# The first six quads of an MLP's up product begin with the two products that need only the first half of the tokens

## The chip, the cores and the metric

The kernel runs on one core of one Trainium2 chip. The metric is device time in microseconds from launch to end. A profile of one execution shows when each engine worked: PE (TensorE, the matmuls), DVE (VectorE), ACT (ScalarE), POOL (GpSimd) and SP (SyncE, which issues most of the transfers).

## The reference

```python
def reference(x, ...):                     # x: 1 x 1024 x 1024, float32
    h = x
    for layer in range(2):
        y = _rms_norm(h, mix_norm_g[layer])
        y = mixer(y)                       # layer 0: chunked spatial gating, layer 1: dilated attention
        h = h + y
        y = _rms_norm(h, mlp_norm_g[layer])
        h = h + jnp.square(jax.nn.relu(y @ w_up[layer])) @ w_down[layer]
    return _rms_norm(h, final_norm_g)
```

There are 1024 tokens and a width of 1024; `w_up` of a layer is 1024 x 4096, `w_down` 4096 x 1024. The change lies in `y @ w_up`, in both layers.

## The kernel before, in words

**Layout and precision.** A tile of activations has 128 features on the partitions and 512 tokens (one half of the tokens) along the free axis, float32, 256 KB. A float32 matrix product is made of three matmuls on rounded parts: `split` has ACT copy a tile into its rounded part (`hi`, L202) and has DVE subtract that from the tile (`lo`, L203); `three` then issues hi x hi, hi x lo and lo x hi into one bank, all through the helper `matmul` at L179. So each tile that TensorE reads costs one ACT and one DVE instruction ahead of it.

**The up product.** The 4096 columns of `w_up` are taken as 16 *quads*, q = 0 to 15. A quad is a 2 x 2 block product: its outputs are two blocks of 128 columns (i) by two halves of the tokens (s), its inputs two halves of the 1024 features (j). A block product ("product" below) has four `three`, one for each 128 features k: 12 matmuls of 128x512. A classical quad needs eight products. The scheme of Strassen and Winograd needs seven, on sums and differences of the blocks:

- Left side, `Weights`: four raw tiles of a quad are loaded on SP's queue into pool tag `r`. POOL makes four sums of them (L357, L358, L359 and L362), and seven pairs (`wp`, eight places) are split from raw tiles and sums. `steps` is a generator that does a piece of this at each call; the call `more()` in the loop over quads sets where the pieces of the next quad stand in each engine's order.
- Right side, `Terms`: `first` makes the eight normed tiles of the first half of the tokens (k = 0 to 7; L397 on DVE, kept in `keep`) and splits each (`y`). `second` makes those of the second half, and for each of the four k the tiles t1 and t2 (products 5 and 6; L416 and L417 on DVE), and on POOL (L418, L419) the tiles from which `rest` splits t3 and t4 (products 7 and 4). Products 1 and 2 read the first half's tiles 0 to 3 and 4 to 7, product 3 the second half's tiles 4 to 7.
- Results: the seven products are added up by ACT and DVE, squared behind a ReLU (`squared`, L654 and L655), combined into seven tiles for the down product (`hidden_terms`) and stored to DRAM on SP's queue (`kept`).

**Quads 0 and 1 are classical.** The sums t1 to t4 need all the tokens, and their norm comes late, since the residual of the second half ends just ahead. So quads 0 and 1 do eight products each: first the four blocks (q, i) on the first half of the tokens in four PSUM banks, tile by tile, then the same on the second half. Each tile is used four times, 12 matmuls. In the mean time `second` and the weights of quad 2 (`up_weights(2)`, all at once) are made. Their eight weights are loaded and split ahead of the MLP (`plain`), in layer 1 in two calls during the attention. From quad 2 on there are seven products, in the order 5, 6, 1, 7, 3, 2, 4.

**What sets the order.** The order of PE's instructions is the order in which the program emits them. Work beside it is emitted by generators that `flow` resumes at a due time: each yields an estimate in ns (`LAT`) of when its result will be there, and `flow.until` resumes them when PE needs it. The other engines' orders come from a list scheduler that goes by the order of emission and by priorities (`tc.high_priority` moves an instruction ahead by 60). PSUM has eight banks: three of tag `mm`, five of tag `at`.

Of the kernel before, what the change touches and what calls it, by code (L numbers as in the profile page):

```python
# [17 lines left out]
P = 128  # L18
# [89 lines left out]
LAT = dict(sum=2600.0, rms=2600.0, tile=1600.0, gate=8500.0, soft=4200.0, turn=3800.0, fe=1300.0, v=2000.0, qk=2700.0, merge=2600.0, out=700.0, fex=3.0, ve=1600.0)  # L108
# [3 lines left out]
def trunk(ctx: ExitStack, tc: tile.TileContext, xT, w_u, w_v, w_o, w_s, b_s, w_qkv, w_bo, rel,  # L112
# [225 lines left out]
    class Weights:  # L338
# [12 lines left out]

        def steps(self):
# [4 lines left out]
            tt(r3, r[0, 0], r[1, 0], op=ALU.subtract)  # L357
            tt(r[1, 0], r[1, 0], r[1, 1], op=ALU.add)  # L358
            tt(r[1, 1], r[1, 0], r[0, 0], op=ALU.subtract)  # L359
            yield  # L360
            self.split(1, r[0, 0])
            tt(r[0, 0], r[0, 1], r[1, 1], op=ALU.subtract)  # L362
            yield
            for p, src in ((5, r[1, 0]), (6, r[1, 1]), (7, r3), (3, r[0, 0]), (2, r[0, 1])):
                self.split(p, src)
                yield

    def ahead(w):

        it = w.steps() if w else iter(())  # L370
        return lambda: next(it, None)

    def plain(layer, q):
        w = {}
        for j in range(2):
            for i in range(2):
                w[i, j] = wpair().split(load(w_up[layer, q, i, j]))
        return w

    class Terms:  # L380


        def __init__(self):
            self.blocks = {(j, s): [] for j in range(2) for s in range(2)}
            self.t = {1: self.blocks[0, 0], 2: self.blocks[1, 0], 3: self.blocks[1, 1], 4: [], 5: [], 6: [], 7: []}
            self.kept = []
# [15 lines left out]
        def second(self, sq, gi):  # L402
# [4 lines left out]
            for k in range(4):  # L407
                y, x, (y0, y1) = [], [], (self.kept[k][:, j, :] for j in range(2))
                for j in range(2):
                    o = 4 * j + k  # L410
                    t = raw()
                    nc.vector.scalar_tensor_tensor(t, h[o][:, sq.cols], vec[:, gi, o:o + 1], pb, op0=ALU.mult, op1=ALU.mult)
# [4 lines left out]
                tt(t2, y[1], t1, op=ALU.subtract)  # L417
                nc.gpsimd.tensor_tensor(y0, y[1], y[0], op=ALU.subtract)  # L418
                nc.gpsimd.tensor_tensor(y1, y1, t2, op=ALU.subtract)  # L419
                yield 2 * LAT["tile"]  # L420
                for j in range(2):
# [181 lines left out]
    for tiles in ((0, 1), (2,), (3,), (4, 5, 6, 7)):  # L603
        w = [weight(w_o[m]) for m in tiles]
        for s in range(2):
# [5 lines left out]
            if tiles[-1] == 7:  # L611
                start_terms(sq[s], s, 1, terms)
                if s == 0:
                    first = [plain(0, q) for q in range(2)]
# [18 lines left out]
    def hidden_terms(q, c11, c21, c12, c22, t2, store=True):  # L633
# [4 lines left out]
        if store:  # L638
            kept(q, {1: c11, 3: c22, 7: t3, 5: c12})
# [7 lines left out]
    def mlp(layer, x, first, last):  # L647


        def up_weights(q):  # L650
            return Weights(lambda i, j: w_up[layer, q, i, j])


        tiles = [(q, i) for q in range(2) for i in range(2)]  # L654
        c = {}  # L655
        for s in range(2):
            banks = [at_bank() if (n < 2) == (s == 1) else mm_bank() for n in range(4)]
            if s == 0:
                banks = [mm_bank() if n < 3 else at_bank() for n in range(4)]
            order = [(j, k) for j in range(2) for k in range(4)] if s == 0 else [(j, k) for k in range(4) for j in range(2)]  # L660
            for n, (j, k) in enumerate(order):
                xs = x.blocks[j, s]
                flow.until(lambda: len(xs) > k)
                for b, (q, i) in zip(banks, tiles):
                    three(b, first[q][i, j], blk(k), xs[k], n == 0, n == 7)
                    flow.pump()
            for b, (q, i) in zip(banks, tiles):
                c[q, i, s] = temp()
                with tc.high_priority(offset=PRIO):
                    squared(c[q, i, s], b)  # L670
                if s and i:
                    hidden_terms(q, c[q, 0, 0], c[q, 1, 0], c[q, 0, 1], c[q, 1, 1], c[q, 0, 0])
            if s == 0:
                w = up_weights(2)
                for _ in w.steps():
                    pass
        x.rest()

        for q in range(2, 16):
# [46 lines left out]
            if q < 14:  # L726
                hidden_terms(q, c11, c21, c12, c22, u)
# [559 lines left out]
    for i in range(2):  # L1287
# [6 lines left out]
        if i == 0:  # L1294
            first = [plain(1, 0)]
# [13 lines left out]
    first.append(plain(1, 1))  # L1309
# [89 lines left out]
```

## Time and profile before

| | us |
|---|---|
| runs, in order | 2202.96, 2199.22, 2202.74 |
| median of the three | 2202.74 |
| profiled execution | 2198.1 |
| its span in the profile | 2196.1 |
| PE busy | 2147.9 (98% of the span) |
| DVE busy | 1560.3 (71%) |
| ACT busy | 1103.5 (50%) |
| POOL busy | 507.8 (23%) |

The profiled execution took 2.0 us more than its span, which runs from the first to the last recorded instruction. All numbers of the trace are from this one execution. In rows of a view in order of time, the first number is when a group of like instructions began (us from the span's start), the second how long the group took, then engine, source line, operation, the tile written and the tiles read, shape and count; in square brackets stands the idle time of that engine ahead of the group, and what ended it. A row of a window has the window, its length, then busy time and number of instructions of PE, PEld (weight load), DVE, ACT and POOL, the granted TensorE clock, the DMA share and GB/s.

### The profile page before, as it was taken

Reading aid. Unit: us, or ns where it says so; the run is one execution under the profiler, and the core shown is the slowest. Engines: PE = TensorE matmul, PEld = TensorE weight load, DVE = VectorE, ACT = ScalarE, POOL = GpSimd, SP = SyncE. Lnnn points to the kernel's source line nnn. Section 1 sums busy time; section 2 is a strip of 40 time slices with the busy share of each in tenths; the row PEclk is TensorE's granted clock in tenths of the full one; section 3 lists DMA queues with packets and bytes.
Section 4 is the critical chain, followed back from the end, with each engine's and each line's share of the span. In section 5 each row is a group of like instructions: output and inputs, shape, how many; then the busy total and the mean of one; then the engine's idle time right before and its main releaser. Section 6 shows DMA issues by size and latency. Waiting matters only on the chain.

```text
span 2196.1 us, 30296 instructions
## 1 busy us (share of the span) xinstructions
PE 2147.9 (98%) x10378; PEld 1775.1 (81%) x10378; DVE 1560.3 (71%) x2851; ACT 1103.5 (50%) x2225; POOL 507.8 (23%) x372
## 2 busy tenths in 40 slices
PE   8999999999999999999999999999999999999997
PEld 6888887888878888778888888887778888788886
DVE  6875278777688887775664745647987777888867
ACT  6644145555564443355544545556555556544432
POOL 1100124333223333510000000001433332333344
PEclk9999999999999999999999999999999999999999
DMA  6321104444355443301111111121154443544432
GB/s 221 112 79 50 39 22 160 159 158 146 123 181 161 153 154 116 106 31 40 44 41 44 35 31 50 31 45 30 39 183 154 154 154 124 192 147 151 149 92 96
DMA packets 152334, 230.27 MB, mean 105 GB/s; under 512 B 32761, under 2 KB 47220, under 8 KB 152180
## 3 DMA queue, kind: packets, MB, share of 16 engines
q1 hardware_dynamic: 151280, 227.11, 33.0%
q8 instruction: 81, 1.33, 0.3%
q10 hardware_dynamic: 900, 1.23, 0.2%
q14 instruction: 73, 0.60, 0.1%
HBM read 170.45 MB, written 57.84 MB: 104 GB/s over the span
## 4 chain that ended last, share of the span: by engine, by line
PE 86%; DVE 7%; ACT 2%; DMA 2%; issue 2%; POOL 1%; SPq 0%; DVEq 0%; POOLq 0%; ACTq 0%
PE mm L179 43%; PE at L179 41%; PE at L186 2%; DVE wp L203 1%; DVE y L203 1%; DMA r<-in_w_v 1%; DVE h L300 0%; DVE t L203 0%; DVE h L791 0%; ACT t L1047 0%; DVE t L1322 0%; ACT wp L202 0%; POOL r L358 0%; POOL t L357 0%; DMA t<-hid 0%
## 5 line engine op out<-in xcount | busy, mean ns | idle before, releaser
L179 PE MATMUL mm<-y,whi 128*128 128x512 f32 x1616 | 508.1, 395 | 1.0 <-DVE h L300 1.0
L202 ACT ACTIVATE wp<-r 128x512 fp32r<-128x512 f32 (+3 forms) x388 | 231.8, 600 | 400.6 <-PE at L179 233.5
L179 PE MATMUL at<-hx,wp 128*128 128x512 f32 x1770 | 416.3, 391 | 1.9 <-DVE h L791 1.8
L179 PEld LDWEIGHTS at<-hx,wp 128*128 128x128 f32 x1770 | 334.2, 189 | 73.3 <-DVE h L791 3.5
L203 DVE TENSOR_TENSOR wp<-r,wp 128x512 fp32r<-128x512 f32 (+3 forms) x388 | 322.7, 835 | 80.2 <-ACT wp L202 77.5
L179 PEld LDWEIGHTS mm<-y,whi 128*128 128x128 f32 x1616 | 296.2, 188 | 62.8 <-DVE h L300 1.4
L179 PE MATMUL mm<-y,wlo 128*128 128x512 f32 x808 | 315.4, 390 | 0.0
L179 PE MATMUL at<-t,wp 128*128 128x512 f32 x1344 | 314.5, 389 | 0.8 <-DVE wp L203 0.7
L179 PEld LDWEIGHTS at<-t,wp 128*128 128x128 f32 x1344 | 252.1, 188 | 53.9 <-DVE wp L203 1.2
L256 POOL TENSOR_TENSOR t<-t 128x512 f32<-128x512 f32 (+1 forms) x66 | 82.6, 1252 | 865.0 <-ACT t L251 853.1
L357 POOL TENSOR_TENSOR t<-r 128x512 f32<-128x512 f32 (+3 forms) x62 | 92.2, 1487 | 607.4 <-DMA r<-in_w_up 181.7
L179 PE MATMUL mm<-y,wp 128*128 128x512 f32 x912 | 223.2, 390 | 0.4 <-DVE y L203 0.2
L179 PEld LDWEIGHTS mm<-y,wp 128*128 128x128 f32 x912 | 171.0, 188 | 37.6 <-issue 0.6
L179 PE MATMUL mm<-hx,wp 128*128 128x512 f32 x708 | 172.2, 390 | 7.8 <-DVE b L812 4.7
L179 PEld LDWEIGHTS mm<-y,wlo 128*128 128x128 f32 x808 | 151.7, 188 | 33.0
L203 DVE TENSOR_TENSOR wlo<-r,whi 128x512 fp32r<-128x512 f32 x160 | 113.9, 734 | 77.9 <-ACT whi L202 77.6
L179 PEld LDWEIGHTS mm<-hx,wp 128*128 128x128 f32 x708 | 132.5, 188 | 37.1 <-ACT wp L202 5.0
L202 ACT ACTIVATE whi<-r 128x512 fp32r<-128x512 f32 x160 | 97.3, 626 | 122.2 <-PE mm L179 91.1
L203 DVE TENSOR_TENSOR hx<-t,hx 128x512 fp32r<-128x512 f32 x192 | 142.1, 743 | 0.5 <-ACT hx L202 0.5
L791 DVE TENSOR_TENSOR h<-h,at 128x512 f32<-128x512 f32 x144 | 97.7, 682 | 57.1 <-PE at L179 57.1
L179 PE MATMUL at<-y,wp 128*128 128x512 f32 x480 | 120.7, 394 | 4.8 <-ACT t L688 4.1
L202 ACT ACTIVATE hx<-t 128x512 fp32r<-128x512 f32 x192 | 119.5, 630 | 6.7 <-DMA t<-hid 2.1
(198 smaller groups left out, 3025.7 us busy)
## 6 DMA issues: line engine op xcount, KB each, us to landing
t<-hid SPq DMA_DIRECT2D x182, 256.0 KB, 3.1
hid<-t SPq DMA_DIRECT2D x140, 256.0 KB, 2.3
r<-in_w_up SPq DMA_DIRECT2D x128, 256.0 KB, 2.7
r<-in_w_dn SPq DMA_DIRECT2D x88, 256.0 KB, 2.6
r<-in_w_qkv SPq DMA_DIRECT2D x72, 256.0 KB, 2.7
hid<-b SPq DMA_DIRECT2D x56, 256.0 KB, 2.4
r<-in_w_v SPq DMA_DIRECT2D x48, 256.0 KB, 3.6
h<-in_xT SPq DMA_DIRECT2D x16, 256.0 KB, 5.6
```

Of the source, the lines that this page charges most:

```text
L179: nc.tensor.matmul(out, lhsT, rhs, **kw)
L186: nc.tensor.transpose(out, src, ident)
L202: nc.scalar.activation(hi, src, AF.Copy)
L203: nc.vector.tensor_tensor(lo, src, hi.bitcast(F32), op=ALU.subtract)
L256: nc.gpsimd.tensor_tensor(self.acc, self.acc, sq, op=ALU.add)
L357: tt(r3, r[0, 0], r[1, 0], op=ALU.subtract)
L791: engine.tensor_tensor(hs[i, s], hs[i, s], src, op=ALU.add)
```

## The change

Quads 0 to 5 (`HEAD = 6`) now begin with products 1 and 2, which read the first half's tiles only.

- `half_first` loads and splits two weights of a quad, (0,0) and (0,1), for products 1 and 2. The callers that called `plain` (two quads of four weights) now call it for quads 0 to 3, with the calls at the same places; quads 4 and 5 follow in the up product.
- Two batches of three quads do product 1 of the three and then product 2 of the three, in the three `mm` banks. Behind product 1 ACT copies the bank out (L696): kept in SBUF for quads 0 and 1, stored to DRAM as `p1` for quads 2 to 5. Product 2 goes on in the same bank; that sum is squared and stored at once.
- The classical quads are gone. Between the batches, four POOL sums each for quads 0 and 1 (`sums`) and then, in a hand-written order, the splits of their weights for products 5, 6, 3, 7 and 4. Products 5 and 6 of both quads run interleaved by k; then each quad does 3, 7 and 4.
- Quads 2 to 5 do five products, 5, 6, 7, 3 and 4, and load product 1 and the finished block back from DRAM. Quads 6 to 15 do seven as before.
- `second` no longer splits the second half's tiles 0 to 3, writes its normed tiles to places of their own (`yr`), emits the splits of t1 and t2 ahead of its wait, with a due time of its own (`terms=6500`), and orders the ACT splits behind the last copy of a bank (`behind`).

```diff
+        def sums(self):
+            r, tt = self.r, nc.gpsimd.tensor_tensor
+            r3 = temp()
+            tt(r3, r[0, 0], r[1, 0], op=ALU.subtract)
+            tt(r[1, 0], r[1, 0], r[1, 1], op=ALU.add)
+            tt(r[0, 0], r[1, 0], r[0, 0], op=ALU.subtract)
+            tt(r[0, 1], r[0, 1], r[0, 0], op=ALU.subtract)
+            self.src = {5: r[1, 0], 6: r[0, 0], 3: r[0, 1], 7: r3, 4: r[1, 1]}
...
+    def half_first(layer, q):
+        return {p: wpair().split(load(w_up[layer, q, 0, j])) for p, j in ((1, 0), (2, 1))}
+    def behind():
+        return tc.issue_after(evacuated[-1]) if evacuated else nullcontext()
...
-                    t = raw()
-                    nc.vector.scalar_tensor_tensor(t, h[o][:, sq.cols], vec[:, gi, o:o + 1], pb, op0=ALU.mult, op1=ALU.mult)
-                    y.append(t)
-                    x.append(pair().split(t))
+                    nc.vector.scalar_tensor_tensor(y[j], h[o][:, sq.cols], vec[:, gi, o:o + 1], pb, op0=ALU.mult, op1=ALU.mult)
...
-                yield 2 * LAT["tile"]
-                for j in range(2):
-                    self.blocks[j, 1].append(x[j])
-                self.t[5].append(pair("t1").split(t1))
-                self.t[6].append(pair("t2").split(t2))
+                with behind():
+                    x, t1, t2 = pair().split(y[1]), pair("t1").split(t1), pair("t2").split(t2)
+                yield LAT["terms"]
+                self.blocks[1, 1].append(x)
+                self.t[5].append(t1)
+                self.t[6].append(t2)
...
+        pre, p1 = [], {}
+        for quads in (range(MMB), range(MMB, HEAD)):
+            banks = [mm_bank() for _ in quads]
+            for p, j in ((1, 0), (2, 1)):
+                xs = x.blocks[j, 0]
+                order = [(k, i) for k in range(4) for i in range(len(quads))]
+                if p == 2 or quads[0]:
+                    order.sort(key=lambda t: t[1])
+                for k, i in order:
+                    q, b = quads[i], banks[i]
+                    flow.until(lambda: len(xs) > k)
+                    three(b, first[q][p], blk(k), xs[k], p == 1 and k == 0, k == 3, skip_group_check=True)
+                    flow.pump()
+                    if k < 3:
+                        continue
+                    t = temp()
+                    with tc.high_priority(offset=PRIO):
+                        if p == 1:
+                            evacuated.append(nc.scalar.activation(t, b, AF.Copy).ins)
+                        else:
+                            squared(t, b)
+                    if p == 2:
+                        kept(q, {1: t})
+                    elif q < 2:
+                        p1[q] = t
+                    else:
+                        kept(q, {"p1": t})
+                if len(first) == 4:
+                    first += [half_first(layer, q) for q in range(4, HEAD)]
+            if not pre:
+                pre.append(up_weights(0))
...
+                pre.append(rest_first(layer, 1, lambda: next(place)))
+        steps = [w.rest() for w in pre]
+        for i in (0, 0, 1, 1, 0, 0, 0, 1):
+            next(steps[i])
+        ds, bs = ([at_bank() for _ in range(2)] for _ in range(2))
+        for k in range(4):
+            flow.until(lambda: len(x.t[6]) > k)
+            for q in range(2):
+                for p, bank in ((5, ds[q]), (6, bs[q])):
+                    three(bank, pre[q][p], blk(k), x.t[p][k], k == 0, k == 3, skip_group_check=True)
+                    flow.pump()
...
-            a = mm_bank()
-            product(a, w[1], x.t[1])
+            u = temp()
+            if q < HEAD:
+                load(hidden_tile(q, "p1"), u)
+            else:
+                a = mm_bank()
+                product(a, w[1], x.t[1])
+                nc.scalar.activation(u, a, AF.Copy)
+            nc.vector.tensor_tensor(u, u, b, op=ALU.add)
             more()
-            u = temp()
-            nc.scalar.activation(u, a, AF.Copy)
-            nc.vector.tensor_tensor(u, u, b, op=ALU.add)
...
-            product(a, w[2], x.t[2], True)
+            c11 = temp()
+            if q < HEAD:
+                load(hidden_tile(q, 1), c11)
+            else:
+                product(a, w[2], x.t[2], True)
+                squared(c11, a)
             more()
-            c11 = temp()
-            squared(c11, a)
```

The new order on PE in layer 1 shows how often a normed tile `y` of the first half is used. Before, each tile is read for four banks (3 matmuls each); these are the tiles 4 to 6:

```order
L179 MATMUL mm_14523<-y_14575,wp_14286 128x512 x3
L179 MATMUL mm_14524<-y_14575,wp_14291 128x512 x3
L179 MATMUL mm_14525<-y_14575,wp_14509 128x512 x3
L179 MATMUL at_14526<-y_14575,wp_14514 128x512 x3
L179 MATMUL mm_14523<-y_14588,wp_14286 128x512 x3
L179 MATMUL mm_14524<-y_14588,wp_14291 128x512 x3
L179 MATMUL mm_14525<-y_14588,wp_14509 128x512 x3
L179 MATMUL at_14526<-y_14588,wp_14514 128x512 x3
L179 MATMUL mm_14523<-y_14619,wp_14286 128x512 x3
```

Now the last tile of product 1 (tile 3, y_14591) is followed by quad 0's product 2, which reads tiles 4, 5, 6 and 7 (y_14620, y_14633, y_14670, y_14703) one behind the other:

```order
L179 MATMUL mm_14569<-y_14591,wp_14326 128x512 x3
L186 MATMUL at_14636<-ident_82,rq_14611 128x128 x4
L179 MATMUL mm_14570<-y_14591,wp_14336 128x512 x3
L179 MATMUL mm_14571<-y_14591,wp_14549 128x512 x3
L179 MATMUL mm_14569<-y_14620,wp_14331 128x512 x3
L179 MATMUL mm_14569<-y_14633,wp_14331 128x512 x3
L179 MATMUL mm_14569<-y_14670,wp_14331 128x512 x3
L179 MATMUL mm_14569<-y_14703,wp_14331 128x512 x3
L179 MATMUL mm_14570<-y_14620,wp_14341 128x512 x3
```

So a tile of 4 to 7 now stands three matmuls behind the one before it, where it stood twelve behind.

The DVE order at the same place decides when those tiles are there. Before, behind tile 5 (y_14588) follow the normed tiles of the second half (r_14596, r_14601) and first sums, with tile 6 (y_14619) in the seventh place and tile 7 (y_14632) in the eleventh:

```order
L203 TENSOR_TENSOR y_14588<-keep_14483,y_14588 128x512
L203 TENSOR_TENSOR y_14598<-r_14596,y_14598 128x512
L412 SCALAR_TENSOR_TENSOR r_14601<-h4_96,vec_80,at_14591 128x512
L416 TENSOR_TENSOR b_14606<-r_14596,keep_14456 128x512
L397 SCALAR_TENSOR_TENSOR keep_14530<-h6_98,vec_80,at_14451 128x512
L203 TENSOR_TENSOR y_14603<-r_14601,y_14603 128x512
L417 TENSOR_TENSOR b_14607<-r_14601,b_14606 128x512
L203 TENSOR_TENSOR y_14619<-keep_14530,y_14619 128x512
L397 SCALAR_TENSOR_TENSOR keep_14544<-h7_99,vec_80,at_14451 128x512
L412 SCALAR_TENSOR_TENSOR r_14641<-h1_93,vec_80,at_14591 128x512
L412 SCALAR_TENSOR_TENSOR r_14646<-h5_97,vec_80,at_14591 128x512
L203 TENSOR_TENSOR y_14632<-keep_14544,y_14632 128x512
```

Now, from the third place behind tile 5 (y_14633), splits of weights (wp) and the first t1 and t2 stand ahead of tile 6 (y_14670) and tile 7 (y_14703):

```order
L439 TENSOR_TENSOR b_14644<-yr_14641,keep_14506 128x512
L203 TENSOR_TENSOR wp_14676<-r_14677,wp_14676 128x512
L440 TENSOR_TENSOR b_14645<-yr_14641,b_14644 128x512
L203 TENSOR_TENSOR y_14650<-yr_14641,y_14650 128x512
L203 TENSOR_TENSOR t1_14653<-b_14644,t1_14653 128x512
L203 TENSOR_TENSOR t2_14656<-b_14645,t2_14656 128x512
L203 TENSOR_TENSOR y_14670<-keep_14575,y_14670 128x512
L203 TENSOR_TENSOR wp_14681<-r_14682,wp_14681 128x512
L203 TENSOR_TENSOR wp_14686<-r_14687,wp_14686 128x512
L422 SCALAR_TENSOR_TENSOR keep_14589<-h7_99,vec_80,at_14501 128x512
L437 SCALAR_TENSOR_TENSOR yr_14725<-h1_93,vec_80,at_14636 128x512
L203 TENSOR_TENSOR y_14703<-keep_14589,y_14703 128x512
```

Tile 6 moved from the seventh to the ninth place behind tile 5, tile 7 from the eleventh to the fourteenth.

On ACT in layer 0, the order of the change around the copies of the second batch's banks (L696; t_3045 is product 1 of quad 3, t_3079 of quad 4), with the splits of the weights for quad 0's products 5 and 6 (wp_3175, wp_3178) and of the second half's tiles and terms (y, t1, t2):

```order
L654 ACTIVATE t_3001<-mm_2824 128x512
L202 ACTIVATE t2_2981<-b_2970 128x512
L655 ACTIVATE t_3001<-t_3001 128x512
L202 ACTIVATE wp_3175<-r_3006 128x512
L202 ACTIVATE wp_3178<-r_3010 128x512
L696 ACTIVATE t_3045<-mm_3030 128x512
L696 ACTIVATE t_3079<-mm_3031 128x512
L202 ACTIVATE y_3067<-yr_3058 128x512
L202 ACTIVATE t1_3070<-b_3061 128x512
```

The copies are new, and the copy of quad 3's bank stands behind two weight splits that wait for POOL's sums.

More of the change, by code (lines that the diff above doesn't have):

```diff
@@ L613, in trunk @@
                 if s == 0:
-                    first = [plain(0, q) for q in range(2)]
+                    first = [half_first(0, q) for q in range(4)]
     hidden = {}
@@ L650, in up_weights @@
         def up_weights(q):
[L651 to L665, printed above, removed]
-                    flow.pump()
[L667 to L676, printed above, removed]
@@ L679, in mlp @@
+        more()
         for q in range(2, 16):
@@ L1294, in trunk @@
         if i == 0:
-            first = [plain(1, 0)]
+            first = [half_first(1, q) for q in range(2)]
         proj_load(3)
```

64 lines of the change are left out of this document (49 added, 15 removed).

## The prediction

> **What bounds the kernel now.** I read the page first (engines, chain), then the chain in order of time, then PE and DVE in order of time where each layer's up product begins.
>
> ```profile
> span 2196.1 us, 30296 instructions
> PE 2147.9 (98%) x10378; PEld 1775.1 (81%) x10378; DVE 1560.3 (71%) x2851; ACT 1103.5 (50%) x2225; POOL 507.8 (23%) x372
> PE 86%; DVE 7%; ACT 2%; DMA 2%; issue 2%; POOL 1%; SPq 0%; DVEq 0%; POOLq 0%; ACTq 0%
> ```
>
> PE is busy for 98% of the span, and 86% of the chain is PE: time is matmuls plus the places where PE waits. In the chain in order of time (start, us, what), one run of matmuls gives the price of a matmul:
>
> ```profile
> 408.56 8.16 PE at L179 x36
> ```
>
> 8.16 / 36 = **0.2267 us** for a 128x512 matmul. So three matmuls (one `three`) are 0.68, a product (12) 2.72, a quad of seven products (84) 19.04, one of five (60) 13.60.
>
> PE in order of time (start, us, what, idle before it and who ended it), layer 0 and then layer 1:
>
> ```profile
> 303.88 2.20 PE L179 MATMUL mm<-y,wp 128*128 128x512 f32 x9
> ...
> 351.93 5.60 PE L179 MATMUL at<-t,wp 128*128 128x512 f32 x24
> ...
> 364.37 3.04 PE L179 MATMUL at<-y,wp 128*128 128x512 f32 x12 [1.40 <-ACT t L688]
> ...
> 427.44 8.32 PE L179 MATMUL at<-t,wp 128*128 128x512 f32 x36
> ```
>
> ```profile
> 1543.55 1.98 PE L179 MATMUL mm<-y,wp 128*128 128x512 f32 x8
> ...
> 1553.32 0.60 PE L186 MATMUL at<-ident,rq 128*128 128x128 f32 x4
> ...
> 1555.15 2.20 PE L179 MATMUL mm<-y,wp 128*128 128x512 f32 x9
> ...
> 1591.87 5.28 PE L179 MATMUL at<-t,wp 128*128 128x512 f32 x22 [0.74 <-DVE wp L203]
> ...
> 1605.30 4.49 PE L179 MATMUL at<-y,wp 128*128 128x512 f32 x12 [2.71 <-ACT t L688]
> ...
> 1669.63 8.32 PE L179 MATMUL at<-t,wp 128*128 128x512 f32 x36
> ```
>
> The last row of each fence is the fourth product of quad 5 (2.72) and then quad 6. From the first up matmul to quad 6, layer 0 takes 430.16 - 303.88 = 126.28 and layer 1 takes 1672.35 - 1543.55 = 128.80, for 528 matmuls (119.7) each. Outside them PE keeps its order, so these two stretches decide. Layer 0 loses 1.40 at quad 2; layer 1 loses 0.74 and 2.71 there, and more behind it:
>
> ```profile
> 1522.00:1525.40 3.40, 3.05 (x15) 2.56 (x16) 2.82 (x6) 2.44 (x4) 1.68 (x2) 1.00 0.00 0
> 626.00:629.40 3.40, 3.15 (x9) 2.51 (x10) 2.97 (x8) 0.94 (x2) 0.00 (x0) 0.63 0.54 165
> 1605.30:1608.70 3.40, 3.40 (x10) 2.70 (x11) 3.40 (x4) 1.63 (x3) 2.28 (x2) 0.68 0.44 156
> ```
>
> ```profile
> 1522.35 0.73 PE L179 MATMUL mm<-o,whi 128*128 128x512 f32 x2 [1.68 <-DVE h L300]
> 626.25 1.06 PE L179 MATMUL mm<-hx,wp 128*128 128x512 f32 x3 [2.13 <-DVE b L812]
> ```
>
> These are stretches right behind a PE wait (granted clock is the third column from the end) and the waits themselves. After 1.68 us of idleness the clock stayed at 1.00; after 2.13 it was 0.63 over 3.4 us, after 2.71 it was 0.68. The twelve matmuls from 1605.30 took 4.3 in place of 2.72. So a wait above about 2.1 costs up to 1.6 more. A rule of the Trainium skill, "TensorE: Matmul & The Clock Gate", section "What's actually happening", puts the half clock behind an idle window of about 3.4 us. The trace is stricter: 2.13 us was enough. By the page alone the waits of 2 to 3 us below would cost nothing more, and my sum would be 1.2 us lower.
>
> **The change, part by part.**
>
> *Matmuls.* Quads 0 and 1 go from eight products to seven: 2 x 12 fewer matmuls a layer, 48 in all (8474 matmuls of 128x512 in the order before, 8426 after): 48 x 0.2267 = **-10.88**, on the bound engine.
>
> *Old waits.* Quad 2 waits at its fifth product (layer 0: 1.40) and in layer 1 at its first (0.74) and fifth (2.71), for splits of weights and normed tiles that all fell into the two classical quads and now lie elsewhere. Layer 0: -1.40, with 0.17 for the restart -1.57. Layer 1: 0.74 + 2.71 + 1.57 for the clock + two restarts, -5.4. Layer 1 also loses time in its first tiles: from 1543.55 to 1555.15 PE does 36 matmuls (8.16) and about 1.2 of sums and transposes in 11.6, so 2.3 of waits, which give way to those below: -2.3. Alone, all this makes -10.88 - 1.57 - 5.4 - 2.3 = -20.1, the floor.
>
> *New work beside PE, each layer.* DVE: six more weight splits, four fewer splits of normed tiles, ten more adds, so +12 instructions; POOL +8; ACT +6; 26 more DMAs of 256 KB on SP (12 weight tiles, 10 loads and 4 stores of hidden tiles). In quads 6 to 15 one weight split a quad stands behind an add that it stood ahead of; nothing there waits, so I cost it at 0. For the rest, three places.
>
> *Layer 1, the first products (the dearest place).* Before, four banks use each normed tile, 12 matmuls or 2.72 us a tile. Now three banks use it in product 1 (2.04), and product 2 of quad 0 alone uses tiles 4 to 7 at 0.68 each. DVE makes them here:
>
> ```profile
> 1551.32 0.69 DVE L203 TENSOR_TENSOR y<-keep,y 128x512 fp32r<-128x512 f32 x1
> ...
> 1554.62 1.29 DVE L203 TENSOR_TENSOR y<-keep,y 128x512 fp32r<-128x512 f32 x2
> ...
> 1560.22 0.68 DVE L203 TENSOR_TENSOR y<-keep,y 128x512 fp32r<-128x512 f32 x1
> ...
> 1562.80 0.68 DVE L203 TENSOR_TENSOR y<-keep,y 128x512 fp32r<-128x512 f32 x1
> ```
>
> ```profile
> 1540.00:1585.00 45.00, 43.85 (x197) 35.46 (x196) 44.20 (x63) 23.77 (x43) 18.20 (x14) 1.00 0.15 48
> ```
>
> These rows are tiles 2, 4 and 5, 6 and 7 of the eight, as the order has them: tile 2 ends at 1552.0, tiles 4 and 5 at 1555.9, tile 6 at 1560.9, tile 7 at 1563.5, and DVE (the fourth figure of the window row) is full: 44.2 of 45 us, 63 instructions of 0.70. In the new DVE order tile 6 stands 9 places behind tile 5 (7 before) and tile 7 stands 14 behind (11 before); the second half's first terms go ahead of them. DVE gets there some 0.3 sooner. Tile 6: 1555.5 + 9 x 0.70 + half a POOL delay = 1562.4; tile 7: 1555.5 + 14 x 0.70 + 0.6 = 1565.9. PE, at two tiles done (18 matmuls, the sums) at 1549.5, waits for tile 2 until 1551.7 in two pieces (about 1.9 in all), then does tile 3, the transposes and tiles 4 and 5 of quad 0 by 1557.2. It waits for tile 6 and again for tile 7, some 7.5 us in all, and starts the last stretch at 1565.9 at half clock (+1.2). The remaining 98 matmuls up to the products 5 and 6 end at 1565.9 + 22.2 + 1.2 + restart 0.2 = **1589.5**. Without waits it would be 1543.55 + 144 x 0.2267 + 1.2 = 1577.4, so the loss is **12.1**. Bounds: DVE with no POOL delay and no clock loss, 9; a full half clock behind each of three waits, 15. By 1589.5 DVE has had time for all that products 5 and 6 of quads 0 and 1 need (25 instructions behind tile 7, 21 us, 1587). From there 360 matmuls, 81.6, and 0.3 restarts: quad 6 at 1671.4 against 1672.35. Layer 1: **-0.9** (by terms -5.44 - 5.4 - 2.3 + 12.1 = -1.0).
>
> *Layer 0, the second batch.* The first half's tiles are all ready when PE arrives, so that wait isn't there. What is new is that POOL makes the weight sums of quads 0 and 1 while it also makes terms:
>
> ```profile
> 312.26 1.41 DVE L412 SCALAR_TENSOR_TENSOR r<-h,vec,at 128x512 f32<-128x512 f32 x2 [2.87 <-PE at L186]
> ...
> 336.81 2.38 DVE L203 TENSOR_TENSOR t<-b,t 128x512 fp32r<-128x512 f32 x2
> ```
>
> ```profile
> L357 POOL TENSOR_TENSOR t<-r 128x512 f32<-128x512 f32 x52 | 82.8, 1592 | 521.0 <-DMA r<-in_w_up 181.7 <-DVE wp L203 124.0 <-DMA r<-in_w_dn 91.7
> ...
> L419 POOL TENSOR_TENSOR keep<-keep,b 128x512 f32<-128x512 f32 x8 | 13.3, 1664 | 7.7 <-DVE b L417 7.7
> ```
>
> From 312.26 to 339.2 DVE did 32 large instructions: 0.84 each. The 14th (second tile of the second half) is done at about 322.7. Five POOL instructions of about 1.59 follow up to the sum for product 6 of quad 0: 330.6, its split on ACT 331.3. In the ACT order the copy of quad 3's product 1 stands behind that split: 331.9. Behind this copy in turn stand that of quad 4 and the terms' splits, for which PE waits next. PE reaches quad 3's product 2, which needs that copy's bank, at 303.88 + 108 x 0.2267 + 2.4 (sums, transposes, one small product) = 330.8: wait **1.1**. Products 5 and 6 start at 341.3; the low half of quad 1's sixth weight is wanted at 343.8, and on DVE comes 17 instructions after 331.9: 17 x 0.76 to 0.84 = 344.8 to 346.2. Wait **1.8**, between 0 and 2.5 (then 1.6 for the clock too). With 0.4 of restarts the new waits are 3.3. Layer 0: -5.44 - 1.57 + 3.3 = **-3.7**.
>
> *The short quads 2 to 5.* A quad now lasts 13.60. One of the old ones:
>
> ```profile
> 400.00:419.04 19.04, 19.04 (x85) 15.77 (x84) 13.62 (x17) 10.09 (x17) 6.32 (x4) 1.00 0.47 152
> ```
>
> DVE 13.62 for 17 instructions, POOL 6.32. A short quad has 14 DVE instructions (five splits, five adds, four terms): 14/17 x 13.62 = 11.2 of 13.60. Weights are split about 8 us ahead of use, since the splits stand behind the adds of the quad before. Loads and stores are 12 x 256 KB in 13.60, 230 GB/s against 152 at a DMA share of 0.47, so 0.7: room. On SP a quad's reload of product 1 stands behind the last store of the quad before and ahead of the weights of the quad two later, so a late store holds those weights back, out of the same 8 us. I cost them at **0**. The cover is 2.4 us a quad; without it, see the second rival.
>
> *Sum:* -0.9 - 3.7 = -4.6 on a span of 2196.1, whose execution took 2198.1: 2193.5. The median of the runs shown is 2202.74, 4.6 above that execution; the same distance gives **2198.2**.
>
> **Rivals.** *Waits small (chance 0.24):* the new waits come in at their lower bounds (9 in layer 1; the copy's 1.1 alone in layer 0). That is -4.0 and -5.9, **2193**. For it: old waits were all under 3 us. Against: the orders, which put the late tiles where I counted them.
>
> *Short quads bound by DVE (0.18), the other side.* Place: quads 2 to 5 of both layers. DVE and POOL hinder each other:
>
> ```profile
> 411.32 0.69 DVE L724 TENSOR_TENSOR t<-t,at 128x512 f32<-128x512 f32 x1 [0.21 <-PE at L179]
> ...
> 412.74 1.77 DVE L640 TENSOR_TENSOR t<-t 128x512 f32<-128x512 f32 x1
> ```
>
> ```profile
> 412.34 1.62 POOL L358 TENSOR_TENSOR r<-r 128x512 f32<-128x512 f32 x1
> ```
>
> An add of two SBUF tiles beside a POOL instruction took 1.77, where one from PSUM took 0.69. If each of the four POOL instructions holds DVE for its whole 1.58, a quad needs 14 x 0.69 + 6.3 = 16.0; it decides from 13.60 on. With the full price 8 x 2.4 = 19; I take the middle, 8 x 1.7 = 14: **2212**. Against it: 17 instructions of 0.69 are 11.7, so four POOL instructions added only 1.9 to the old quad. The Trainium skill, "SBUF — State Buffer", section "SBUF: two separate sides", states that full price: the port pair that DVE and GpSimd share is an exclusive lock, and the loser blocks for the whole instruction. The trace agrees for single rows (1.77), not for the quad's sum.
>
> *Half clock everywhere (0.12):* each of three more waits is followed by 1.6 of half clock: -4.6 + 4.8, **2203**.
>
> **How the numbers follow.** The forecast has 0.46, with its own range 2194 to 2202. Faster or slower by 0.2% is 4.4 us, about what a measurement of this kernel can tell. Of the forecast 0.23 lies beyond 4.4 and 0.23 within; with the rivals, faster 0.23 + 0.24 = 0.47; same 0.23 + 0.12 = 0.35; slower 0.18. The range, 2188 to 2211, takes in the small waits down to their bounds and most of the slow short quads.
>
> **What would show it.** Right: 48 fewer matmuls; in layer 1 two PE waits in quad 0's second product, named for a DVE y, adding to 5 to 9 us, then half clock; in layer 0 a wait for an ACT copy of 1 or 2 us; old waits at L688 gone; short quads of 13.6. Wrong: short quads above 14, PE waits for wp or DMA in them, or layer 1's tiles 6 and 7 before 1560.

## The result, and the profile after

The changed kernel is **slower**: median 2221.1 us of 5 runs (2217.55 to 2226.4) against 2200.15 of 5 runs of the kernel before (2198.81 to 2202.96), ratio **1.0101** with a 95% interval of 1.0088 to 1.0115. The forecast was 2198.2 in a range of 2188 to 2211. The profiled execution took 2221.73 us, its span 23.9 us more than that of before, where I had forecast 4.6 less: 28.5 us to explain. The page of the changed kernel:

```profile
span 2220.0 us, 30355 instructions
PE 2149.7 (97%) x10330; PEld 1769.6 (80%) x10330; DVE 1578.3 (71%) x2875; ACT 1106.0 (50%) x2237; POOL 537.5 (24%) x388
PE 79%; DVE 10%; DMA 4%; ACT 3%; issue 3%; POOL 1%; SPq 0%; DVEq 0%; POOLq 0%; ACTq 0%
```

PE has 48 instructions fewer, as counted, and yet more busy time: matmuls at half clock. The share of PE in the chain fell from 86% to 79%; DVE (7% before) and DMA (2%) have grown. PE in order of time, layer 0:

```profile
306.46 3.56 PE L179 MATMUL mm<-y,wp 128*128 128x512 f32 x15
...
335.85 2.67 PE L179 MATMUL mm<-y,wp 128*128 128x512 f32 x6 [2.37 <-ACT t L696]
...
348.23 6.28 PE L179 MATMUL at<-t,wp 128*128 128x512 f32 x27
...
366.67 0.50 PE L179 MATMUL at<-t,wp 128*128 128x512 f32 x1 [1.50 <-ACT t L202]
368.89 0.73 PE L179 MATMUL at<-t,wp 128*128 128x512 f32 x2 [1.72 <-DVE t L203]
371.29 5.49 PE L179 MATMUL at<-t,wp 128*128 128x512 f32 x12 [1.68 <-DVE t L743]
...
383.26 11.22 PE L179 MATMUL at<-t,wp 128*128 128x512 f32 x48 [0.78 <-DVE t L743]
...
440.65 8.50 PE L179 MATMUL at<-t,wp 128*128 128x512 f32 x36 [1.33 <-DVE t L785]
```

and layer 1:

```profile
1556.25 1.98 PE L179 MATMUL mm<-y,wp 128*128 128x512 f32 x8
...
1574.89 0.54 PE L179 MATMUL mm<-y,wp 128*128 128x512 f32 x1 [2.82 <-ACT y L202]
1577.20 1.22 PE L179 MATMUL mm<-y,wp 128*128 128x512 f32 x2 [1.76 <-DVE y L203]
1579.72 25.57 PE L179 MATMUL mm<-y,wp 128*128 128x512 f32 x99 [1.30 <-ACT y L202]
1605.13 11.04 PE L179 MATMUL at<-t,wp 128*128 128x512 f32 x48
...
1626.37 4.62 PE L179 MATMUL at<-t,wp 128*128 128x512 f32 x12 [1.67 <-DVE t L743]
...
1637.21 11.22 PE L179 MATMUL at<-t,wp 128*128 128x512 f32 x48 [0.79 <-DVE t L743]
...
1694.58 8.46 PE L179 MATMUL at<-t,wp 128*128 128x512 f32 x36 [1.80 <-DVE t L785]
```

I cut each up product into three stretches: **first products** (from the first row to products 5 and 6 at 348.23 and 1605.13, 144 matmuls), **quads 0 and 1** (the next 120 matmuls; the rows at 383.26 and 1637.21 hold quad 1's product 4 and then quad 2, so the stretch ends 2.72 behind their start), and **quads 2 to 5** (240 matmuls, to 2.72 behind the start of the rows at 440.65 and 1694.58). The forecast for quads 0 and 1 of layer 0 is what its total for that layer, 126.28 - 3.7 = 122.6, leaves beside the other two.

| us | forecast, layer 0 | measured | forecast, layer 1 | measured |
|---|---|---|---|---|
| first products | 37.4 | 41.8 | 45.95 | 48.9 |
| quads 0 and 1 | 30.8 | 37.8 | 27.5 | 34.8 |
| quads 2 to 5 | 54.4 | 57.4 | 54.4 | 57.4 |

The differences are 4.4 + 7.0 + 3.0 and 2.9 + 7.3 + 3.0, 27.6 us of the 28.5. The rest lies outside: 2.6 more ahead of the first up matmul (306.46 against 303.88), where the change does nothing, and 1.6 less between and behind the two up products. Over the twelve kernels of the experiments that start lies between 303.75 and 309.33.

### The profile page after: what moved, and what is told of

It reads as the page before. It is cut to its first block, busy times and chain, and to the rows that moved or that the text cites. A ratio compares the mean times of both kernels' runs of the same rounds, so it can differ in the third digit from the quotient of the medians.

```text
span 2220.0 us, 30355 instructions
## 1 busy us (share of the span) xinstructions
PE 2149.7 (97%) x10330; PEld 1769.6 (80%) x10330; DVE 1578.3 (71%) x2875; ACT 1106.0 (50%) x2237; POOL 537.5 (24%) x388
## 4 chain that ended last, share of the span: by engine, by line
PE 79%; DVE 10%; DMA 4%; ACT 3%; issue 3%; POOL 1%; SPq 0%; DVEq 0%; POOLq 0%; ACTq 0%
PE mm L179 41%; PE at L179 36%; PE at L186 2%; DVE wp L203 2%; DMA r<-in_w_v 1%; DMA t<-hid_p 1%; DVE h L872 1%; DVE t L203 1%; DMA r<-in_w_up 1%; ACT t L654 1%; DVE t L664 1%; DVE h L300 0%; DMA t<-in_w_dl 0%; ACT t L1128 0%; DVE t L661 0%
## 5 line engine op out<-in xcount | busy, mean ns | idle before, releaser
L179 PE MATMUL at<-t,wp 128*128 128x512 f32 x1536 | 364.6, 393 | 14.0 <-DVE t L743 4.9
L179 PEld LDWEIGHTS at<-t,wp 128*128 128x128 f32 x1536 | 290.1, 190 | 80.6 <-DVE t L743 6.6
L372 POOL TENSOR_TENSOR t<-r 128x512 f32<-128x512 f32 (+3 forms) x54 | 78.3, 1450 | 556.2 <-DMA r<-in_w_dn 187.5
L179 PE MATMUL mm<-y,wp 128*128 128x512 f32 x768 | 192.1, 402 | 9.8 <-ACT y L202 5.2
L179 PEld LDWEIGHTS mm<-y,wp 128*128 128x128 f32 x768 | 148.1, 194 | 46.1 <-ACT y L202 6.8
L179 PEld LDWEIGHTS mm<-hx,wp 128*128 128x128 f32 x708 | 132.5, 188 | 36.7 <-ACT wp L202 5.0
L1128 ACT ACTIVATE t<-t,st 128x128 f32<-128x128 f32 (+1 forms) x192 | 84.2, 440 | 68.3 <-DVE st L1126 68.2
```

What stands on the lines that cost most here:

```text
L179: nc.tensor.matmul(out, lhsT, rhs, **kw)
L1128: nc.scalar.activation(p[:, c], p[:, c], AF.Exp, bias=m, scale=-1.0, accum_out=dn)
```

## The experiments

The theories: (1) quads 0 and 1 are late because DVE, slowed by POOL's sums through a shared port, is not done with the terms and weights when PE gets there, since less of PE's work stands ahead of them than before; (2) quads 2 to 5 wait for a round trip through DRAM. Rivals: the sums or the places of buffers are late, not DVE; the short quads have too much DVE work or too many transfers; the waits come from a bank that is read and written in turn. Ratios are against the kernel before; 0.001 is 2.2 us. Stretches are of each kernel's profiled execution, in the order layer 0, layer 1, to be set beside the table above.

Two cautions. The intervals of the changed kernel and of the single edits are 0.002 to 0.005 wide, up to 10 us, so a gain of a few us is read from the stretches, not from the total. And a stretch is one execution: the early-load kernel has the changed kernel's order up to quad 2, and its first products took 43.9 and 50.1 (41.8 and 48.9 in the changed kernel), its quads 0 and 1 34.1 and 34.5 (37.8 and 34.8). So 3 or 4 us of one stretch of layer 0 say little by themselves.

**Early load of product 1.** The load of `p1` is issued ahead of the stores of the quad before (the lines are for quads 3 to 5; quad 2's load is moved in the same way in the loop over quads 0 and 1):

```diff
...
             squared(c21)
+            if q + 1 < HEAD:
+                ready[q + 1] = load(hidden_tile(q + 1, "p1"), temp())
             if q < 14:
                 hidden_terms(q, c11, c21, c12, c22, u, without=(1,) if q < HEAD else ())
```

> Quads 2 to 5 load product 1 ahead of the stores of the quad before, nothing else changes. Loop theory (each of these quads waits for a round trip: last store of the quad before, load of product 1 behind it on SP's queue, adds, squares, last store): the four quads take 54.4 us a layer where they took about 57.4, so about -6 us in all. Rival 1 (DVE with POOL's lock bounds them): less than 1 us. Rival 2 (the transfers themselves are too many): less than 1 us, and the loads land as late as before.

Ratio 1.0071 (1.0048 to 1.0095), about 6.6 us won by the ratios; the stretches of quads 2 to 5 give 5.8. In the changed kernel, the chain of waits through quad 3 in order of time (start, us, what) shows the round trip:

```profile
404.61 1.65 DVE wp L203
406.26 0.62 DVE b L666
...
406.89 0.32 SPq L650
...
407.26 2.70 DMA t<-hid_p
...
410.06 0.69 DVE t L778
410.74 0.61 DVE t L785
```

The last combination (L666) goes to the store on SP (L650), the load behind it on the same queue lands 2.7 us later, and then come the adds (L778, L785) whose results end in the next quad's L666. Such stores were issued at 406.89, 420.81 and 436.03: 13.9 and 15.2 us a turn against 13.60 of matmuls. With the early load, PE in order of time in layer 0:

```profile
392.71 11.04 PE L179 MATMUL at<-t,wp 128*128 128x512 f32 x48
403.60 2.88 PE L179 MATMUL at<-y,wp 128*128 128x512 f32 x12
406.31 11.04 PE L179 MATMUL at<-t,wp 128*128 128x512 f32 x48
417.19 2.88 PE L179 MATMUL at<-y,wp 128*128 128x512 f32 x12
```

403.60 to 417.19 is one quad: 13.59. Quads 2 to 5 take 54.5 and 54.5. DVE, POOL and the transfers have the same work as in the changed kernel, so none of them bounds the short quads: the order of loads and stores on SP's queue does. Theory 2 is shown.

**Product 2 tile by tile in the first batch.**

```diff
-                if p == 2 or quads[0]:
+                if quads[0]:
                     order.sort(key=lambda t: t[1])
```

> In the first batch product 2 runs tile by tile over its three quads, as product 1 does, so that 18 more matmuls (4.1 us) stand ahead of tile 7. Theory of late tiles (what layer 1 loses in the first batch is lost for good): -4 us. Rival (DVE is full from there to the end of quad 1, and sets when that ends, so what is won is waited for later): layer 1's PE waits before products 5 and 6 get smaller by 3 to 4 us, those behind them larger by as much, and the time changes by less than 1 us.

Ratio 1.0084 (1.0067 to 1.0100), 3.7 us won, which the intervals alone don't tell from nothing. The total is near the first theory's, the way to it is not: in layer 1 the first products take 41.7 where they took 48.9, and quads 0 and 1 39.0 where they took 34.8; in layer 0 38.4 (41.8) and 41.2 (37.8). So 7.2 is won and 4.2 given back, and in layer 0 3.4 for 3.4. Where it is given back, layer 1:

```profile
1604.25 1.60 PE L179 MATMUL at<-t,wp 128*128 128x512 f32 x3 [2.87 <-DVE wp L203]
1608.83 11.37 PE L179 MATMUL at<-t,wp 128*128 128x512 f32 x37 [2.98 <-DVE wp L203]
```

PE came to product 5 sooner and stood twice for a weight split that DVE had not done. So the rival is right for more than half of layer 1, and layer 0 fits it.

**Sums left out, and sums that nobody reads.** The first kernel drops the eight POOL sums of quads 0 and 1 in each layer and splits raw tiles; the second keeps POOL's work but lets it write into a spare tile, as these lines of its diff show (`bare` is true for quads 0 and 1; the first kernel drops these three sums and the one ahead of them):

```diff
...
-            tt(r[1, 0], r[1, 0], r[1, 1], op=ALU.add)
-            tt(r[0, 0], r[1, 0], r[0, 0], op=ALU.subtract)
-            tt(r[0, 1], r[0, 1], r[0, 0], op=ALU.subtract)
-            self.src = {5: r[1, 0], 6: r[0, 0], 3: r[0, 1], 7: r3, 4: r[1, 1]}
+            tt(r3 if bare else r[1, 0], r[1, 0], r[1, 1], op=ALU.add)
+            tt(r3 if bare else r[0, 0], r[1, 0], r[0, 0], op=ALU.subtract)
+            tt(r3 if bare else r[0, 1], r[0, 1], r[0, 0], op=ALU.subtract)
+            self.src = {5: r[1, 0], 6: r[0, 0], 3: r[0, 1], 7: r[1, 1] if bare else r3, 4: r[1, 1]}
```

> The eight POOL sums of quads 0 and 1 (16 in both layers) are left out: raw weight tiles take their place, so the output is not the reference's. Theory of the shared port (a DVE instruction beside a POOL one takes 1.77 us in place of 0.69, and DVE is full there): DVE is through some 6 to 9 us earlier in each layer, and of the waits up to quad 2, about 13 and 10 us, two thirds go: -12 to -18 us. Rival (it is DVE's own instructions that fill it, and the places of buffers): -3 us or less.

> POOL still makes the eight sums of quads 0 and 1 of each layer, but into a tile that nobody reads; raw weight tiles are split in their place, so the output is not the reference's. It splits what leaving the sums out won (layer 0: 5.8 us ahead of products 5 and 6 and 4.0 behind them; layer 1: 0.1 and 5.6). If it was the shared port: DVE is as slow as in the changed kernel, and within 3 us of its time is all that is left. If it was the lateness of the sums (splits wait for them, and copies of banks behind those splits on ACT): nearly all of the 15 us is won here too, and DVE's instructions are as long as in the changed kernel.

Left out: ratio 1.0032 (1.0020 to 1.0044), 15 us won; first products 36.0 and 48.8, quads 0 and 1 33.7 and 29.2. Unread: 1.0105 (1.0081 to 1.0128), nothing won; 36.7 and 48.8, 40.7 and 35.0. The windows of layer 1 from DVE's first term of the second half to its last split of a term (busy time and instructions of PE, PEld, DVE, ACT, POOL) for the changed kernel, the one without sums and the one with unread sums:

```profile
1569.40:1625.70 56.30, 47.19 (x186) 36.23 (x184) 54.25 (x60) 33.30 (x61) 33.51 (x21) 0.91 0.35 112
```

```profile
1558.70:1610.90 52.20, 46.38 (x186) 36.31 (x184) 47.11 (x60) 32.86 (x61) 23.99 (x13) 0.90 0.35 121
```

```profile
1568.20:1624.90 56.70, 47.30 (x186) 36.19 (x184) 54.65 (x60) 32.90 (x61) 33.33 (x21) 0.91 0.34 112
```

DVE has the same 60 instructions in all three, splits of raw tiles standing for splits of sums. With 13 POOL instructions they take 47.11, with 21 they take 54.25, and 54.65 when nobody waits for these eight: 7.1 to 7.5 us, or **0.9 us of DVE for each POOL sum**. Which instructions get slower shows in the changed kernel, on DVE and on POOL:

```profile
1594.50 1.78 DVE L203 TENSOR_TENSOR wp<-r,wp 128x512 fp32r<-128x512 f32 x1
...
1601.30 1.39 DVE L437 SCALAR_TENSOR_TENSOR yr<-h,vec,at 128x512 f32<-128x512 f32 x2
```

```profile
1593.99 1.74 POOL L356 TENSOR_TENSOR t<-wr 128x512 f32<-128x512 f32 x1
...
1600.90 1.63 POOL L359 TENSOR_TENSOR wr<-wr 128x512 f32<-128x512 f32 x1
```

The split reads two SBUF tiles and takes 1.78 beside a POOL sum; the two normed tiles, which read a PSUM bank (`at`), take their usual 0.7 each. So it is in the whole window: the 22 DVE instructions on two SBUF tiles without a POOL instruction beside them took 0.68 to 0.69, and of the 25 that overlap one by more than 0.2 us, 15 took 1.76 to 1.80; the six that read a bank stayed at 0.68 to 0.74 beside POOL.

In layer 1, then, quads 0 and 1 are late because POOL's work slows DVE, which is what the theory of the shared port says, and not because the sums come late. DVE is slowed in layer 0 too: from the first term of the second half to the last split of a term it is busy for 52.60 in the changed kernel and 44.20 without the sums, again for 60 instructions. But the first products of layer 0 are the other way round: both kernels win their 5 us (with POOL's sums the same order took 41.8, 43.9 with the early load and 40.2 with the pairs), so there it was the lateness (the copy of quad 3's bank stood behind a split that waited for a sum; its wait of 2.37 is 0 and 0.39). How much of quads 0 and 1 of layer 0 is which stays open, since the unread kernel can't be read there: ACT stood 4.6 and 8.5 us for the tile into which POOL wrote, a wait that only this edit has.

**The sums on DVE.** (`sums` takes the engine.)

```diff
...
-        w.sums()
+        w.sums(nc.vector if q < 2 else nc.gpsimd)
```

> DVE in place of POOL makes the eight sums of quads 0 and 1 of each layer. Theory of the shared port: a POOL sum costs the DVE instruction beside it 1.08 us (1.77 in place of 0.69), a sum on DVE itself 0.69, so DVE has 3 us less to do in each layer, and the sums come without POOL's 1.6 us each: of the waits up to quad 2 go 3 to 6 us a layer, -4 to -10 us in all. Rival (DVE's own count of instructions fills it): 8 x 0.69 = 5.5 us more a layer, up to +11 us.

Ratio 1.0090 (1.0075 to 1.0105), at best 2.4 us won and not clear of noise, below what I expected and far from the rival's +11. The same window of layer 1, beside those above:

```profile
1565.80:1622.40 56.60, 47.88 (x185) 37.38 (x184) 52.31 (x67) 32.92 (x61) 25.43 (x13) 0.88 0.32 112
```

The 67 instructions are the 60 with eight sums more and one add fewer: 47.11 + 7 x 0.69 = 51.9 against 52.31. So a sum costs DVE about 0.7 when DVE makes it, and 0.9 when POOL does.

**Nine quads with the first products.**

```diff
...
-    HEAD = 6
+    HEAD = 9
-        for quads in (range(MMB), range(MMB, HEAD)):
+        for quads in (range(q, q + MMB) for q in range(0, HEAD, MMB)):
```

(with the weights of quads 6 to 8 loaded behind the second batch's product 1, and the sums of quads 0 and 1 behind the second batch)

> Nine quads begin with products 1 and 2, in three batches: 72 more matmuls (16.3 us) stand ahead of products 5 and 6 in each layer, beside six more weight splits on DVE (4 to 6 us). Theory of cover (PE comes to quads 0 and 1 before DVE is through): of the waits behind the first products, about 10 and 8 us, nearly all go, while three more short quads a layer cost 0.8 us each: -10 to -15 us. Rival (the loss lies in the short quads or in the order of the splits, not in how early PE comes): no change or up to 5 us more.

Ratio 1.0064 (1.0046 to 1.0083), 8.1 us won, a little less than the theory's 10 to 15. Quads 0 and 1 take 29.2 and 29.2 where they took 37.8 and 34.8, so the cover does what it should. Only these waits are left there, layer 0:

```profile
382.54 3.01 PE L179 MATMUL at<-t,wp 128*128 128x512 f32 x12 [0.78 <-DVE t L743]
...
391.78 11.17 PE L179 MATMUL at<-t,wp 128*128 128x512 f32 x48 [0.78 <-DVE t L743]
```

That is the bank: product 4 goes on in product 7's bank right behind it, while DVE still adds from it (L743). These waits are the 2.0 us above the 27.2 of 120 matmuls; where the pairs below take them away as well, 27.2 is measured. In layer 1 a copy of a bank is late by 2.5 in the third batch, with the half clock behind it: 4 us of the gain are lost there.

**Pairs.** Quads 0 and 1 run 3 and 3, 7 and 7, 4 and 4 (three short loops in place of one, no other edit).

> Quads 0 and 1 run their last products in pairs: 3 and 3, 7 and 7, 4 and 4, so that product 4 no longer stands right behind product 7 of its own bank. Theory of the bank (the waits of 0.78 to 1.68 us for the add at that place come from the bank alone): these four waits go, and product 7's tiles have 2.7 us more, 2 to 4 us a layer, -4 to -8 us. Rival (DVE is full up to the end of quad 1, and its end stays): the waits move to other products of quads 0 and 1, and the change is below 2 us.

Ratio 1.0102 (1.0086 to 1.0118), nothing won. Quads 0 and 1 take 31.6 and 27.9, 6 and 7 us less, and quads 2 to 5 62.4 and 63.3 where they took 57.4. One row of layer 0 holds it:

```profile
392.52 12.76 PE L179 MATMUL at<-t,wp 128*128 128x512 f32 x48 [4.58 <-DVE t L789]
```

The rival was right: while DVE is behind, taking a wait away only moves it.

**All together.** The four edits (early load, tile by tile, nine quads, pairs), and these with the sums on DVE:

> Together: nine quads with the first products, the early load, product 2 of the first batch tile by tile, and the pairs. If the losses are apart, as the theories have it (loop 6, late tiles 4, cover 10 with three more short quads at full pace, bank 3), this stands 20 to 26 us below the changed kernel, 0.2% or more below the kernel before. Rival (they are one loss, DVE's, that each edit only moves): about the time of the best single edit, 8 us below the changed kernel.

> The same with the sums of quads 0 and 1 on DVE. With the cover of nine quads PE no longer waits for DVE there, so by the theory of the shared port only the waits for copies of banks that stand behind POOL's sums on ACT (2.4 us in layer 0, 2.5 in layer 1) go: -2 to -5 us against the four edits. By the rival (DVE's count) 0 to +6 us.

Ratios 0.9994 (0.9982 to 1.0005) and 0.9987 (0.9976 to 0.9997): 23 and 25 us below the changed kernel, as the theories of separate losses have it, but only level with the kernel before, where they had it 0.2% below. The sums on DVE bring 1.5 us at most, not clear of noise, where I expected 2 to 5. Quads 0 and 1 run in 27.2 and 27.2, without a wait. Two losses are left: the first products of layer 1, 60.9 us for 216 matmuls (49.0), and the fifth product of quad 2. The second, on PE in layer 0, and DVE ahead of it:

```profile
402.58 11.22 PE L179 MATMUL at<-t,wp 128*128 128x512 f32 x48 [3.20 <-DVE t L791]
```

```profile
387.68 0.69 DVE L661 TENSOR_TENSOR t<-t 128x512 f32<-128x512 f32 x1 [1.17 <-DMA t<-hid]
...
392.86 0.97 DVE L661 TENSOR_TENSOR t<-t 128x512 f32<-128x512 f32 x1 [1.96 <-DMA t<-hid]
```

DVE, with quad 2's adds queued behind it, waits for the reload of quads 0 and 1's finished blocks. So the next kernel loads these two blocks ahead of the fourth products; the one after it also gives the first half's normed tiles priority (`tc.high_priority` in `first`), and a third one moves the sums to DVE too:

```diff
...
+        c11s = [load(hidden_tile(q, 1), temp()) for q in range(2)]
         for q, wq in enumerate(pre):
             product(es[q], wq[4], x.t[4], True)
```

> The four edits, and the finished blocks of quads 0 and 1 are loaded ahead of their fourth products, so that the combinations of these quads no longer wait for the load (1.2 and 2.0 us on DVE in layer 0 of the four edits). Theory: DVE comes to quad 2's adds 2 to 3 us sooner, the waits of 3.2 and 2.3 us at quad 2's fifth product go with their restarts, -4 to -7 us against the four edits. Rival (DVE is full there without that load too): less than 1.5 us.

> The same, and the first half's normed tiles and their splits have priority on DVE and ACT. Theory of late tiles: in layer 1 the waits in the first batch (4.8 us and the half clock behind them, about 10 us lost against 216 matmuls) shrink by 4 to 7 us, and with nine quads of cover it is not given back. Rival (the second half's norm and terms come later by as much, and products 5 and 6 wait for them): less than 2 us.

> The same with the sums of quads 0 and 1 on DVE. As between the four and the five edits: 0 to -2 us.

With the early blocks the ratio is **0.9966 (0.9954 to 0.9978)**, some 7.5 us below the kernel before, and the waits at that place have shrunk to 1.32 and 0.66:

```profile
401.36 11.20 PE L179 MATMUL at<-t,wp 128*128 128x512 f32 x48 [1.32 <-DVE t L791]
...
1641.32 11.18 PE L179 MATMUL at<-t,wp 128*128 128x512 f32 x48 [0.66 <-DVE t L791]
```

The priority gave this back: 0.9994 (0.9985 to 1.0003), and 0.9992 (0.9981 to 1.0003) with the sums on DVE. Its layer 1 begins so, on PE and on DVE:

```profile
1545.07 1.59 PE L179 MATMUL mm<-y,wp 128*128 128x512 f32 x3 [2.94 <-ACT y L202]
1547.03 2.50 PE L179 MATMUL mm<-y,wp 128*128 128x512 f32 x5 [0.36 <-DVE h L300]
```

```profile
1544.25 0.67 DVE L300 TENSOR_TENSOR h<-h,mm 128x512 f32<-128x512 f32 x1
...
1546.29 1.28 DVE L300 TENSOR_TENSOR h<-h,mm 128x512 f32<-128x512 f32 x2
```

The up product starts 3.1 us later (1545.07 against 1541.93 with the early blocks) and its first products take 60.2 against 60.5. Neither theory said so. The first tile itself comes no later: ACT's split of it is done at about 1539.5 in both kernels. What comes later are the last three residual adds (L300), which read the `mm` banks that the up product writes next. With the early blocks they start at 1540.43 and 1542.23; here the tiles with priority stand ahead of them, the first of the three ends at 1544.92, and PE starts 0.15 behind it. So the wait for tiles was exchanged for a wait for banks. The name in the row of 1545.07 misleads, since the split that it names had long been done; I read the bank from the order of times, and from the next wait, which names L300.

## Why the prediction was wrong, point by point

- **Matmuls, old waits.** Right: 48 matmuls are gone, and so are the waits at quad 2's first and fifth product.
- **Layer 1, the first products.** The mechanism was right: waits for tiles in quad 0's second product. They are 2.82 + 1.76 + 1.30 = 5.9 where I had 7.5. Mis-sized was the half clock: the 99 matmuls from 1579.72 took 25.6, 3.1 over their price, where I had 1.2, and the 11 matmuls from 1564.51, behind the waits for tile 2, took 4.4, 1.9 over, where I had nothing. The stretch is 2.9 longer than forecast.
- **Layer 0, the second batch.** The wait for the copy behind weight splits is there, 2.37 for 1.1; the wait of 1.8 for quad 1's sixth weight is not. Again the half clock is the larger part; below.
- **Quads 0 and 1: the step that failed.** "From there 360 matmuls, 81.6, and 0.3 restarts": I checked DVE up to products 5 and 6 and took products 3, 7 and 4 behind them as covered. "For the rest, three places" left out this fourth one, worth 14.3 us in this execution. The larger part is DVE's lateness, the smaller the bank that product 4 shares with product 7 (2.0 us a layer by the nine quads). DVE's window in layer 1 before, from the second half's first term to the last split of a term:

```profile
1553.90:1602.90 49.00, 47.95 (x211) 39.02 (x209) 46.61 (x61) 28.95 (x53) 21.48 (x15) 1.00 0.31 102
```

Against 54.25 for 60 now. DVE has no more instructions there than before (the twelve I counted lie elsewhere or took the place of others); it has six more POOL instructions beside it. And 186 matmuls stand beside this work where 211 did: at 0.2267, 42 us for 56 where there were 48 for 49. Both sides moved the wrong way, and I had added up neither. The kernel without sums shows the one side, the nine quads the other.
- **Short quads 2 to 5: costed at 0, cost 6.0.** I had seen that the reload stands behind the last store on SP, and let it hold back only weights with 8 us of lead. The load itself has no lead: it is wanted at once. The early load shows it, 54.5 a layer.
- **Rivals.** The slow short quads came in with 6 of their 14 us, by the round trip and not by DVE. The price of the shared port that I set aside there is part of what makes quads 0 and 1 late. My argument against it was the old quad, where four POOL instructions added 1.9; DVE had room there. The Trainium skill, "SBUF — State Buffer", section "SBUF: two separate sides", says that the loser blocks for the whole instruction. The runs agree with it better than I did: a POOL sum cost DVE 0.9 us on average, most of the 1.08 that a single blocked row (1.77 in place of 0.69) shows.

## What to carry to other kernels

For every engine that works ahead of the bound one, add up its work from where it may start to where its last result is wanted, and the bound engine's work over the same distance, before and after; a change that shortens the one and lengthens the other can turn a hidden engine into the bound with no instruction more on it. A reload that stands behind a store on one queue closes a loop: issue the load first. While an engine is behind, taking away one wait only moves it, so the edits that keep all the work won 0 to 8 us each; four of them together came level with the kernel before, and only with the early blocks was it passed, by 7.5 us.

## What the runs showed of the hardware

The half clock lasts longer than I priced, and comes sooner. Windows of 3.4 us behind layer 0's wait of 2.37 in the changed kernel (granted clock is the third column from the end):

```profile
335.85:339.25 3.40, 3.40 (x8) 1.71 (x8) 3.37 (x5) 1.46 (x3) 2.54 (x3) 0.55 0.69 163
339.25:342.65 3.40, 3.40 (x9) 2.25 (x8) 3.40 (x3) 1.12 (x3) 3.40 (x3) 0.50 0.38 146
342.65:346.05 3.40, 3.40 (x16) 2.78 (x15) 3.40 (x5) 1.11 (x3) 3.32 (x3) 0.95 0.20 77
```

Two windows at 0.55 and 0.50: 3.4 x (0.45 + 0.50) = 3.2 us behind one wait of 2.37, twice the 1.6 that I had read off the trace of before as the most. Of the 4.4 us that layer 0's first products are over the forecast, this and the longer wait are nearly all.

I had read a limit of about 2.1 us for a wait that brings the half clock. In the kernel with the four edits one wait of 1.81, with none in the ten us ahead of it, was enough; and in layer 1 of the changed kernel four short waits were, of 0.19, 0.52, 1.13 and 0.25 within 6.3 us. PE and a window behind its wait for each, the four edits first:

```profile
1563.77 30.43 PE L179 MATMUL mm<-y,wp 128*128 128x512 f32 x125 [1.81 <-DVE y L203]
1564.80:1568.20 3.40, 3.40 (x9) 2.17 (x8) 3.37 (x6) 0.63 (x1) 0.00 (x0) 0.52 0.47 154
```

```profile
1564.51 4.38 PE L179 MATMUL mm<-y,wp 128*128 128x512 f32 x11 [0.25 <-DVE y L203]
1563.80:1567.20 3.40, 3.15 (x8) 2.30 (x9) 3.40 (x8) 1.89 (x3) 0.00 (x0) 0.67 0.10 37
```

So waits that follow each other closely count together, and a wait has to be priced with its neighbours.

A GpSimd add of 128x512 cost DVE 0.9 us where DVE was full, more than the 0.7 of doing it there.
